# Operand pieces, background pieces, squares and first weights moved to other places in a two-layer trunk kernel

## The chip, the cores and the metric

The kernel runs on one core of a Trainium2 chip. The metric is the device time of one execution in microseconds (us). Engines go by the profile's names: PE is TensorE (PEld is its weight load), DVE is VectorE, ACT is ScalarE, POOL is GpSimd, SP is SyncE, which here issues the DMAs.

## The reference, cut to what matters

Two transformer-like layers over 1024 prompt tokens and 8 x 8 sample tokens, model width 1024, all in float32:

```
h = x
for layer in (0, 1):
    hn = rms_norm(h, norm_mix_g[layer])
    # layer 0: causal conv (width 31, LayerNorm, silu) | stick-breaking attention
    # layer 1: gated short conv                        | multi-scale causal pooling
    h = h + mixer(hn @ w_in) @ w_out
    g, u = split(rms_norm(h, norm_ffn_g[layer]) @ w_ffn_in[layer])      # 1024 -> 2 x 2816
    h = h + (silu(g) * u) @ w_ffn_out[layer]                            # 2816 -> 1024
y = rms_norm(h, norm_final_g)
```

The sample tokens have a cache of 1024 positions for the attention, gathered by a page table. Keys, values and the states of the convolutions and the pooling are outputs as well.

## The kernel before, in words

Activations lie transposed: channels on the partitions, tokens along the free axis. The 1088 tokens are two column groups, GA (0 to 511) and GB (512 to 1087, 576 columns). `hb` holds the residual stream in eight chunks of 128 channels.

**Matmuls.** Each float32 product is three products of split operands (high by high, high by low, low by high; `mm3`, L235). A *block* is one output chunk of 128 channels: eight input chunks of three products. PE does little else, and every block reads a 512 KB piece of weights that comes from memory just in time.

**Weights.** `w_load` (L166) has SP fetch a piece into `stage` (four buffers). `w_split` makes from it `hl` (three buffers): the high half by one ACT instruction (L184), the low half by two POOL subtractions (L186). In the FFN of group GB some pairs of channel pieces go by Strassen's scheme, seven products in place of eight; there DVE first forms sums of weights (L200 to L202), and ACT and POOL split those (L196, L197). `w_next` takes a piece and calls both for later ones.

**Order.** Nothing is scheduled by a tool; each engine runs its instructions in the order in which the code issues them. So that PE never waits, smaller work is put between its matmuls by hand. After each input chunk of a block a *slot* is called, and a slot takes the next piece of some other work:

- In layer 0, while GA goes through output projection (`run_out`) and FFN (`run_ffn`), slots take *background* pieces (`bg` from the list `flow`): the attention of GB (scores `z` L991, transposes `m` L1020, weighted sums `o` L1030 on PE; `q`, `be`, `kt` on DVE, L1005 to L1010 and L968; exponentials and copies on ACT), then the attention of the sample tokens and the convolution of GB. `drain` finishes what is left after GA's FFN.
- In layer 0, while GB goes through its FFN, slots take 21 *jobs* (`p0` to `p4` for four chunks, and a last cut), which form the sums and differences of GB's activations for the Strassen blocks: DVE lines L1466 to L1500, with a split of each by ACT and POOL (L1471). Once they are done, slots take pieces of the next layer's input (`ahead`) or GA's squares (`slot_d`). Those slots lie inside a block (`block(..., slot=slot)`, three a block), after a block (`slot()` in `one`), and between the blocks of the FFN's second matrix (`out_block`, 1.6 us each, which add to `hb` by DVE, L297).
- In layer 1, while GA goes through the FFN, every third slot takes a step of `forms_b`, which normalizes GB for its own FFN.

**The end of an output projection.** `run_out` does two chunks in a `pair` first, then four blocks, then chunks 6 and 7 in a `pair`. In this last pair each step also scales one finished chunk of `hb` for the FFN (`prep`: ACT L381, DVE L384 into `x`). `fin(n)` adds chunk n to `hb` (DVE L297) and its square to `ss` (`add_squares`: ACT L251, POOL L252). `norm_a` and `norm_b` make the root mean square's reciprocal from `ss`; the FFN's results are scaled by it afterwards (`rr`, DVE L293).

**A plain FFN block** ends in `acc` (PSUM, three buffers in GB's FFN). DVE scales it into `tmp` (L293), ACT applies silu, POOL or DVE multiplies, and ACT and DVE split the result into `hid` (L241).

**The start.** SP loads four pieces of x into `xt`; PE transposes them into `m` (L699), DVE copies them to `hb` (L705), ACT casts them (L381). The first weight is cast by ACT (L184) behind the first of these.

Of the kernel before, what the change touches and what calls it, by code (L numbers as in the profile page):

```python
# [57 lines left out]
def trunk_kernel(ctx, tc, x_prompt, x_sample, cache_k, cache_v, state_conformer, state_shortconv, state_pool,  # L58
# [261 lines left out]

    def pair(g, accs, x, ks, hooks, slot=None, skew=0, early=None):
        st = ((accs(), w_next()), (accs(), w_next(1)))
        for i in range(KC + skew):
            for (a, h), j in zip(st, (i, i - skew)):
                if 0 <= j < KC:
                    k = ks[j]
                    mm3(g, a, h[:, 0, k], h[:, 1, k], x[k], j == 0, j == KC - 1)
            if early and i == KC - 1:  # L330
                early(st[0][0])
            if i < skew:
                continue
            for f in hooks.get(k, []):
                f()
            if slot and j < KC - 1:
                slot()
        return st[0][0], st[1][0]

# [52 lines left out]
    def run_out(g, accs, x, gcol, ks=K0, slot=lambda: None, then=None):  # L392
        then = then or (g, x)

        def fin(n, a):
            added(g, hb[:, n, g.cs], a)
            add_squares(g, hb[:, n, g.cs], n == 0)

        a0, a1 = pair(g, accs, x, ks, {ks[0]: [flush]}, slot)
        w_split(wj[0] + 3)  # L400
        fin(0, a0)
        fin(1, a1)
        for n in range(2, 6):
            slot()
            h = w_next()
            a = accs()
            block(g, a, h, x, ks, slot=slot)
            w_split(wj[0] + 3)
            fin(n, a)
        slot()  # L410
        a0, a1 = pair(g, accs, x, K0, {k: [lambda k=k: prep(*then, k, pc(gcol + k)), lambda: low(0)]
                                       for k in range(6)}, slot, skew=2, early=lambda a: fin(6, a))
        w_split(wj[0] + 3)
        for n, a in ((6, a0), (7, a1)):
            if n == 7:
                fin(n, a)
            prep(*then, n, pc(gcol + n))
            low(1)
        low()
# [38 lines left out]


    def run_ffn(g, accs, ps, hidp, x, last, sig=False, slot=lambda: None, forms=None, plain=NF,  # L460
                free=lambda: None, hw=None, both=True):
        G = NF // 2
        n = g.n
        hid = {}
# [43 lines left out]
        def one(f, which):  # L508
            h = w_next()
            a = accs()  # L510
            block(g, a, h, x, K0[4:] + K0[:4] if done else K0, slot=slot)
            flush()
            ev_g(a) if which == 0 else ev_u(f, a)
            slot()
# [146 lines left out]
    def load_x(hf, t):  # L661
# [4 lines left out]
        else:  # L666
            sp.dma_start(xt[hf, t][:64], x_sample.rearrange("b q c -> (b q) c")[:, c])

    for hf in range(2):
        for t in range(4):  # L670
            load_x(hf, t)
        w_load(2 + hf)
# [752 lines left out]
    def slot_d():  # L1425
        turn[0] += 1
        if sq and turn[0] % 4 == 0:
            n = sq.pop(0)
            add_squares(GA, hb[:, n, GA.cs], n == 0)
# [21 lines left out]


    def make_forms(g, fp, gcol):
        def wide():
            assert "a" not in sums
            return fp.tile([128, 1024], F, name="sum1024")

        w2 = g.n // 2
        n1, n2 = slice(g.c0, g.c0 + w2), slice(g.c0 + w2, g.c1)
        l, r = slice(0, w2), slice(w2, g.n)  # L1460
        xs = [fp.tile([128, 3 * w2], F, name=f"xs{k}") for k in range(4)]
        tt = [[fp.tile([128, 2, g.n], FR, name=f"tt{k}_{i}") for i in range(2)] for k in range(4)]
        jobs = []

        def normed(out, c, cs):
            dve.scalar_tensor_tensor(out, hb[:, c, cs], pc(gcol + c), rr[:, cs], op0=OP.mult, op1=OP.mult)  # L1466

        def cut(k, i, x):
            o = tt[k][i]
            act.activation(o[:, 0], x[:, :g.n], AF.Copy)  # L1470
            pool.tensor_tensor(o[:, 1], x[:, :g.n], f32(o[:, 0]), op=OP.subtract)  # L1471

        box = {}

        def job(k):
            b21, b22, b11 = xs[k][:, l], xs[k][:, r], xs[k][:, g.n:]

            def p0():
                if k:
                    cut(k - 1, 1, box["u"])  # L1480
                normed(xs[k][:, 0:g.n], k + 4, g.cs)

            def p1():
                normed(b11, k, n1)

            def p2():
                t = box["t"] = tmp()
                normed(t[:, r], k, n2)
                dve.tensor_tensor(t[:, l], t[:, r], b11, op=OP.subtract)

            def p3():
                t, u = box["t"], wide()
                box["u"] = u
                dve.tensor_tensor(u[:, l], b22, t[:, r], op=OP.subtract)
                dve.tensor_tensor(t[:, r], b22, t[:, l], op=OP.subtract)

            def p4():
                t, u = box["t"], box["u"]
                cut(k, 0, t)
                dve.tensor_tensor(u[:, r], b21, t[:, r], op=OP.subtract)  # L1500
            return [p0, p1, p2, p3, p4]

        for k in range(4):
            jobs += job(k)
        jobs.append(lambda: cut(3, 1, box["u"]))

        def switch():
            while jobs:
                jobs.pop(0)()
            for k in range(4):  # L1510
                split(x1[4 + k][:, :, l], xs[k][:, g.n:])
            for k in range(4):
                split(x1[k][:, :, :g.n], xs[k][:, 0:g.n])

        forms = {"b21": lambda k: x1[k][:, :, l], "b22": lambda k: x1[k][:, :, r], "b11": lambda k: x1[4 + k][:, :, l],
                 "switch": switch}
        for i, (a, b) in enumerate((("t1", "t2"), ("t3", "t4"))):
            forms[a] = lambda k, i=i: tt[k][i][:, :, l]
            forms[b] = lambda k, i=i: tt[k][i][:, :, r]
        return forms, jobs  # L1520

    with tc.tile_pool(name="hid0b", bufs=2) as hidp:
# [17 lines left out]
        def slot_f():  # L1540
            if ahead:
                return ahead.pop(0)()
            if not jobs or wj[0] < jstart:
                return slot_d()
            jobs.pop(0)()

        jstart = wj[0] + 3
        run_ffn(GB, accs, ms, hidp, x1, to_mixer, slot=slot_f, forms=forms, plain=PLAIN, free=early)

    acc_pool(GT, 2)  # L1550

# [147 lines left out]

    def out_fin(g, n, a):  # L1700
        added(g, hb[:, n, g.cs], a)
        add_squares(g, hb[:, n, g.cs], n == 0)

    def normed(out, c, cs, view=lambda ap: ap):
        dve.scalar_tensor_tensor(out, view(hb[:, c, cs]), pc(FFNG + 8 + c), view(rr[:, cs]), op0=OP.mult, op1=OP.mult)
# [83 lines left out]


    def forms_b():
        dg = norm_a(GB, ms, D, xs[3])
        yield 1
        yield 1
        norm_b(GB, ms, dg)
        yield 1
        for k in range(4):
            normed(xs[k][:, 0:GB.n], k + 4, GB.cs)
            yield 1
            normed(xs[k][:, GB.n:], k, GB.cs)  # L1800
            yield 1
# [232 lines left out]
```

## Time and profile before

| | |
|---|---|
| time, median of three runs | 2506.31 us (2504.49 to 2506.65) |
| the profiled execution's own time | 2507.39 us |
| its span, first to last instruction | 2505.6 us |
| PE busy | 2420.9 us of the span |
| DVE, POOL, ACT busy | 1653.7, 1625.1, 1106.5 us |
| mean granted TensorE clock | 0.994 |

Times in the profile's rows are microseconds from the start of the span. In a row of the timeline come start, duration, engine, line, operation, output and inputs with their shapes, the count, and in brackets the idle time of the engine just before, with what ended it. In a row of windows come the window, its length, the busy time and count of PE, PEld, DVE, ACT and POOL, the granted clock, the share of the DMA engines and GB/s. The output projection of GA in layer 0 lies at about 330 to 430 us, the plain blocks of GB's FFN in layer 0 from about 1020, the output projection of GB in layer 1 ends at about 1728.

### The profile page before, as it was taken

The page shows a single profiled execution, that of the slowest core. Times are in us where ns is not written, and L with a number is a line of the kernel's source. Part 1 is how long each engine was busy: PE and PEld are TensorE (multiplying, and loading weights), DVE is VectorE, ACT ScalarE, POOL GpSimd, SP SyncE. Part 2 cuts the span into 40 slices and gives each one's busy share as a digit, 9 for nine tenths or more (in the row PEclk, how much of TensorE's full clock was granted, in tenths as well). Part 3 has the DMA queues.
Part 4 walks back from the last instruction along what each step waited for, and adds up shares of the span by engine and source line. Part 5 has one row for each costly group of instructions (what it writes and reads, how often), then busy time and mean ns, then how long its engine had stood idle before and what let it go on. Part 6 is the DMA issues. An engine that isn't in the chain of part 4 may idle for free.

```text
span 2505.6 us, 41453 instructions
## 1 busy us (share of the span) xinstructions
PE 2420.9 (97%) x15877; PEld 2190.0 (87%) x15877; DVE 1653.7 (66%) x2288; ACT 1106.5 (44%) x1877; POOL 1625.1 (65%) x1264
## 2 busy tenths in 40 slices
PE   8999999999999999999999999998999999999998
PEld 6788877788777679999999999888888888999998
DVE  3696878977777553766566534458777668666655
ACT  5536876754444343343333422234333444443333
POOL 6764334655654576787787523267888886887775
PEclk9999999999999999999999999999999999999999
DMA  7332231234565534223232311242233323233322
GB/s 226 117 108 73 77 111 48 72 103 144 175 180 172 160 93 148 71 74 98 89 100 86 111 49 43 71 139 68 85 101 102 98 90 92 85 98 114 93 85 81
DMA packets 355485, 258.31 MB, mean 103 GB/s; under 512 B 22913, under 2 KB 303617, under 8 KB 355272
## 3 DMA queue, kind: packets, MB, share of 16 engines
q1 hardware_dynamic: 355256, 255.66, 34.5%
q8 instruction: 126, 2.06, 0.3%
q14 instruction: 71, 0.58, 0.1%
q10 hardware_dynamic: 32, 0.01, 0.0%
HBM read 237.41 MB, written 18.69 MB: 102 GB/s over the span
## 4 chain that ended last, share of the span: by engine, by line
PE 73%; DVE 16%; POOL 4%; issue 3%; ACT 3%; DMA 1%; SPq 0%; DVEq 0%; ACTq 0%; POOLq 0%
PE acc L235 44%; PE acc L525 20%; DVE sum L200 1%; POOL hl L197 1%; DVE hb L297 1%; DVE q L1008 1%; POOL hl L186 1%; PE o L1030 1%; DVE hid L241 1%; PE m L1020 1%; PE m L1132 1%; PE z L991 1%; DVE sum L201 1%; PE z L1155 1%; DVE cacc L831 1%
## 5 line engine op out<-in xcount | busy, mean ns | idle before, releaser
L186 POOL TENSOR_TENSOR hl<-stage,hl 128x512 fp32r<-128x512 f32 x464 | 637.8, 1399 | 389.3 <-ACT hl L184 280.9
L235 PE MATMUL acc<-x,hl 128*128 128x512 f32 (+1 forms) x3648 | 773.5, 350 | 11.2 <-DVE tmp L293 3.0
L235 PEld LDWEIGHTS acc<-x,hl 128*128 128x128 f32 x3648 | 587.9, 190 | 75.1 <-issue 5.8
L235 PE MATMUL acc<-hid,hl 128*128 128x288 f32 (+1 forms) x3096 | 548.2, 333 | 10.8 <-DVE tmp L293 4.6
L235 PEld LDWEIGHTS acc<-hid,hl 128*128 128x128 f32 x3096 | 471.0, 189 | 62.9 <-DVE hb L297 7.2
L297 DVE TENSOR_TENSOR hb<-acc,hb 128x512 f32<-128x512 f32 (+1 forms) x360 | 256.3, 718 | 173.1 <-PE acc L235 171.7
L525 PE MATMUL acc<-x,hl 128*128 128x288 f32 (+1 forms) x2676 | 361.9, 290 | 3.0 <-POOL hl L197 2.4
L525 PEld LDWEIGHTS acc<-x,hl 128*128 128x128 f32 x2676 | 348.6, 188 | 5.3 <-POOL hl L197 3.3
L197 POOL TENSOR_TENSOR hl<-sum,hl 128x512 fp32r<-128x512 f32 x180 | 237.7, 1349 | 169.3 <-ACT hl L196 169.3
L184 ACT ACTIVATE hl<-stage 128x1024 fp32r<-128x1024 f32 x232 | 243.8, 1054 | 228.6 <-PE acc L235 145.8
L529 DVE TENSOR_TENSOR tmp<-acc,tmp 128x288 f32<-128x288 f32 (+1 forms) x420 | 173.6, 441 | 230.6 <-ACT tmp L541 136.2
L197 POOL TENSOR_TENSOR hl<-stage,hl 128x512 fp32r<-128x512 f32 x180 | 268.4, 1513 | 14.4 <-ACT hl L196 14.4
L525 PE MATMUL acc<-b,hl 128*128 128x256 f32 (+1 forms) x1548 | 215.7, 290 | 14.1 <-DVE tmp L529 11.2
L525 PEld LDWEIGHTS acc<-b,hl 128*128 128x128 f32 x1548 | 201.3, 188 | 19.8 <-ACT hl L196 12.6
L235 PE MATMUL acc<-x1t,hl 128*128 128x288 f32 x1152 | 216.3, 296 | 1.5 <-POOL hl L186 1.5
L235 PEld LDWEIGHTS acc<-x1t,hl 128*128 128x128 f32 x1152 | 195.9, 188 | 19.5 <-POOL hl L186 1.8
L196 ACT ACTIVATE hl<-sum 128x512 fp32r<-128x512 f32 x180 | 103.0, 623 | 238.1 <-DVE sum L202 217.6
L293 DVE TENSOR_TENSOR tmp<-acc,rr 128x512 f32<-128x512 f32 (+1 forms) x108 | 75.2, 710 | 136.3 <-PE acc L235 122.4
L196 ACT ACTIVATE hl<-stage 128x512 fp32r<-128x512 f32 x180 | 105.5, 618 | 69.4 <-PE acc L235 59.3
L504 POOL TENSOR_TENSOR tmp<-tmp 128x576 f32<-128x576 f32 (+1 forms) x85 | 126.2, 1485 | 9.2 <-ACT tmp L481 8.2
L252 POOL TENSOR_TENSOR ss<-ss,tmp 128x512 f32<-128x512 f32 (+1 forms) x69 | 108.1, 1566 | 25.5 <-ACT tmp L251 15.2
L235 PE MATMUL acc<-x1a,hl 128*128 128x512 f32 x480 | 121.7, 407 | 2.5 <-POOL hl L186 1.3
(298 smaller groups left out, 3166.5 us busy)
## 6 DMA issues: line engine op xcount, KB each, us to landing
stage<-in_w_ffn_in_dram SPq DMA_DIRECT2D x176, 512.0 KB
stage<-in_w_ffn_out_dram SPq DMA_DIRECT2D x88, 512.0 KB
stage<-in_w_in_even_dram SPq DMA_DIRECT2D x40, 512.0 KB
kst<-in_cache_k_dram SPq DMA_DIRECT2D x64, 256.0 KB
vst<-in_cache_v_dram SPq DMA_DIRECT2D x56, 256.0 KB
stage<-in_w_out_even_dram SPq DMA_DIRECT2D x16, 512.0 KB
stage<-in_w_in_odd_dram SPq DMA_DIRECT2D x16, 512.0 KB
stage<-in_w_out_odd_dram SPq DMA_DIRECT2D x16, 512.0 KB
```

What stands on the lines that cost most here:

```text
L184: act.activation(hl[:, 0], st, AF.Copy)
L186: pool.tensor_tensor(hl[:, 1, c], st[:, c], f32(hl[:, 0, c]), op=OP.subtract)
L196: act.activation(hl[:, 0, c], x, AF.Copy)
L197: pool.tensor_tensor(hl[:, 1, c], x, f32(hl[:, 0, c]), op=OP.subtract)
L200: todo = [lambda: dve.tensor_tensor(sb, su[:, lo], su[:, hi], op=OP.add), lambda: dve.tensor_tensor(sa[:, hi], sg[:, lo], su[:, lo], op=OP ...
L235: pe.matmul(acc[:, b, :c1 - c0], w, xs[:, xi, c0 - o:c1 - o], start=first and s == 0, stop=last and s == 2)
L252: pool.tensor_tensor(ss[:, g.cs], ss[:, g.cs], t[:, :g.n], op=OP.add)
L293: dve.tensor_tensor(d, a, r, op=OP.mult)
L297: dve.tensor_tensor(d, a, d, op=OP.add)
L504: (dve if both and f == NF - 1 else pool).tensor_tensor(t[:, :n], t[:, :n], u[:, :n], op=OP.mult)
L525: pe.matmul(acc[:, :w2], h[:, wi, i, k], xk[:, xi], start=k == 0 and s == 0, stop=k == 3 and s == 2)
L529: dve.tensor_tensor(out, acc[:, :w2], x, op=OP.add)
```

## The change

Five edits:

1. The first weight piece is loaded ahead of x: SP now issues one `stage` load, four of `xt`, a `stage`, four of `xt`, a `stage`, where four of `xt` came first and then two `stage` loads. The orders of ACT, DVE, POOL and PE at the start stay.
2. In the last pair of `run_out`, background pieces are taken in the first four steps and no longer in the last three (`quiet=3`). The three pieces come that much later, and all background behind them shifts by three slots.
3. In the same pair `sixth` issues the weight split of the piece after next ahead of `fin(6)`.
4. In the FFN of GB in layer 0 the jobs are taken only inside plain blocks (`inner=slot_j`); slots after a block or in the FFN's second matrix take other work. The jobs' scratch tile (`wide`) is now a part of `ss`.
5. In layer 1 the squares of GB's chunks 4 to 7 are left out of the output projection; `forms_b` does them, one in every third slot, from its second step on. `norm_a` and everything else in `forms_b` comes fifteen slots later.

```diff
-    def pair(g, accs, x, ks, hooks, slot=None, skew=0, early=None):
+    def pair(g, accs, x, ks, hooks, slot=None, skew=0, early=None, quiet=0):
...
-            if slot and j < KC - 1:
+            if slot and j < KC - 1 - quiet:
                 slot()
@@ run_out
+        def sixth(a):
+            w_split(wj[0] + 2)
+            fin(6, a)
...
         a0, a1 = pair(g, accs, x, K0, {k: [lambda k=k: prep(*then, k, pc(gcol + k)), lambda: low(0)]
-                                       for k in range(6)}, slot, skew=2, early=lambda a: fin(6, a))
+                                       for k in range(6)}, slot, skew=2, early=sixth, quiet=3)
@@ run_ffn, in one()
-            block(g, a, h, x, K0[4:] + K0[:4] if done else K0, slot=slot)
+            block(g, a, h, x, K0[4:] + K0[:4] if done else K0, slot=inner or slot)
@@ the start
+    w_load(1)
     for hf in range(2):
         for t in range(4):
             load_x(hf, t)
@@ make_forms
-        def wide():
-            assert "a" not in sums
-            return fp.tile([128, 1024], F, name="sum1024")
+        wide = ss[:, g.cs]
@@ FFN of GB, layer 0
         def slot_f():
             if ahead:
                 return ahead.pop(0)()
-            if not jobs or wj[0] < jstart:
-                return slot_d()
-            jobs.pop(0)()
+            slot_d()
+
+        def slot_j():
+            if jobs and wj[0] >= jstart:
+                jobs.pop(0)()
+            else:
+                slot_f()
@@ out_fin, layer 1
         added(g, hb[:, n, g.cs], a)
-        add_squares(g, hb[:, n, g.cs], n == 0)
+        if g is GA or n < 4:
+            add_squares(g, hb[:, n, g.cs], n == 0)
@@ forms_b
+        yield 1
+        for n in range(4, KC):
+            add_squares(GB, hb[:, n, GB.cs], False)
+            yield 1
         dg = norm_a(GB, ms, D, xs[3])
```

ACT at the end of GA's output projection in layer 0, before: `L996`, `L965`, `L966` and `L1021` are background, `L381` scales a chunk, `L251` squares one, and `L184` casts a weight.

```order
L996 ACTIVATE q_4165<-z_4160,bh 128x1024
L996 ACTIVATE be<-z_4160,bh 128x1024
L965 ACTIVATE kt<-kall 64x1024
L966 ACTIVATE qa<-hb 64x512
L251 ACTIVATE tmp<-hb 128x512
L381 ACTIVATE x_5_76<-hb,par 128x512
L1021 ACTIVATE wt_4190<-m 128x512
L1021 ACTIVATE wt_4190<-m 128x128
L996 ACTIVATE q_4205<-z_4200,bh 128x896
L996 ACTIVATE be<-z_4200,bh 128x896
L184 ACTIVATE hl<-stage 128x1024 x2
```

The same place after the change:

```order
L381 ACTIVATE x_4_75<-hb,par 128x512
L184 ACTIVATE hl<-stage 128x1024
L251 ACTIVATE tmp<-hb 128x512
L381 ACTIVATE x_5_76<-hb,par 128x512
L184 ACTIVATE hl<-stage 128x1024
L381 ACTIVATE x_6_77<-hb,par 128x512
L251 ACTIVATE tmp<-hb 128x512
L381 ACTIVATE x_7_78<-hb,par 128x512
```

The background's rows are gone from between the last scalings, and one weight cast stands ahead of the square and scaling of the sixth chunk.

DVE in the FFN of GB in layer 0, before: `L293` evacuates a plain block, `L1466` to `L1500` are jobs, `L241` splits a hidden piece, `L297` evacuates the eight parts of the second matrix.

```order
L1466 SCALAR_TENSOR_TENSOR xs_10840<-hb,par,rr 128x576
L1466 SCALAR_TENSOR_TENSOR xs_10840<-hb,par,rr 128x288
L1466 SCALAR_TENSOR_TENSOR tmp<-hb,par,rr 128x288
L1489 TENSOR_TENSOR tmp<-tmp,xs_10840 128x288
L1494 TENSOR_TENSOR sum_11307<-xs_10840,tmp 128x288
L1495 TENSOR_TENSOR tmp<-xs_10840,tmp 128x288
L293 TENSOR_TENSOR tmp<-acc,rr 128x576
L1500 TENSOR_TENSOR sum_11307<-xs_10840,tmp 128x288
L241 TENSOR_TENSOR hid<-tmp,hid 128x576
L293 TENSOR_TENSOR tmp<-acc,rr 128x576
L297 TENSOR_TENSOR hb<-acc,hb 128x576 x8
```

After the change (job lines are now L1468 to L1501):

```order
L1468 SCALAR_TENSOR_TENSOR xs_10840<-hb,par,rr 128x576
L1468 SCALAR_TENSOR_TENSOR xs_10840<-hb,par,rr 128x288
L1468 SCALAR_TENSOR_TENSOR tmp<-hb,par,rr 128x288
L1491 TENSOR_TENSOR tmp<-tmp,xs_10840 128x288
L241 TENSOR_TENSOR hid<-tmp,hid 128x576
L293 TENSOR_TENSOR tmp<-acc,rr 128x576
L297 TENSOR_TENSOR hb<-acc,hb 128x576 x8
L200 TENSOR_TENSOR sum_11514<-stage 128x512
L201 TENSOR_TENSOR sum_11513<-stage 128x512
L202 TENSOR_TENSOR sum_11513<-sum_11514,stage 128x512
L1495 TENSOR_TENSOR ss<-xs_10840,tmp 128x288
L1496 TENSOR_TENSOR tmp<-xs_10840,tmp 128x288
```

The last three jobs of the fourth chunk now come behind the eight parts of the second matrix, and four job rows stand between two evacuations where six stood.

POOL at the end of GB's output projection in layer 1, before: `L252` adds a square to `ss`, `L186` and `L197` make the low halves of weights.

```order
L252 TENSOR_TENSOR ss<-ss,tmp 128x576
L186 TENSOR_TENSOR hl<-stage,hl 128x512 x2
L252 TENSOR_TENSOR ss<-ss,tmp 128x576
L197 TENSOR_TENSOR hl<-sum_17599,hl 128x512 x2
L252 TENSOR_TENSOR ss<-ss,tmp 128x576
L197 TENSOR_TENSOR hl<-sum_17600,hl 128x512
L197 TENSOR_TENSOR hl<-stage,hl 128x512
L252 TENSOR_TENSOR ss<-ss,tmp 128x576
L197 TENSOR_TENSOR hl<-stage,hl 128x512 x2
L252 TENSOR_TENSOR ss<-ss,tmp 128x576
L197 TENSOR_TENSOR hl<-sum_c,hl 128x512
```

After, further on in the FFN of GA (L508 there is a product of hidden values):

```order
L252 TENSOR_TENSOR ss<-ss,tmp 128x576
L197 TENSOR_TENSOR hl<-stage,hl 128x512 x2
L508 TENSOR_TENSOR tmp<-tmp 128x512
L197 TENSOR_TENSOR hl<-sum_c,hl 128x512
L186 TENSOR_TENSOR hl<-stage,hl 128x512 x4
L252 TENSOR_TENSOR ss<-ss,tmp 128x576
L508 TENSOR_TENSOR tmp<-tmp 128x512
L197 TENSOR_TENSOR hl<-sum_18249,hl 128x512 x2
L252 TENSOR_TENSOR ss<-ss,tmp 128x576
L197 TENSOR_TENSOR hl<-sum_18250,hl 128x512
L197 TENSOR_TENSOR hl<-stage,hl 128x512
L252 TENSOR_TENSOR ss<-ss,tmp 128x576
```

The four squares that stood between the last weights of the projection now stand between weights of the FFN.

More of the change, by code (lines that the diff above doesn't have):

```diff
@@ L460, in run_ffn @@
     def run_ffn(g, accs, ps, hidp, x, last, sig=False, slot=lambda: None, forms=None, plain=NF,
-                free=lambda: None, hw=None, both=True):
+                free=lambda: None, hw=None, both=True, inner=None):
         G = NF // 2
@@ L1479, in p0 @@
                 if k:
-                    cut(k - 1, 1, box["u"])
+                    cut(k - 1, 1, wide)
                 normed(xs[k][:, 0:g.n], k + 4, g.cs)
@@ L1491, in p3 @@
             def p3():
-                t, u = box["t"], wide()
-                box["u"] = u
+                t, u = box["t"], wide
                 dve.tensor_tensor(u[:, l], b22, t[:, r], op=OP.subtract)
@@ L1497, in p4 @@
             def p4():
-                t, u = box["t"], box["u"]
+                t, u = box["t"], wide
                 cut(k, 0, t)
@@ L1504, in make_forms @@
             jobs += job(k)
-        jobs.append(lambda: cut(3, 1, box["u"]))
+        jobs.append(lambda: cut(3, 1, wide))
         def switch():
@@ L1542, in slot_f @@
                 return ahead.pop(0)()
-            if not jobs or wj[0] < jstart:
-                return slot_d()
-            jobs.pop(0)()
+            slot_d()
[4 more added lines that the diff above has]
+                slot_f()
         jstart = wj[0] + 3
-        run_ffn(GB, accs, ms, hidp, x1, to_mixer, slot=slot_f, forms=forms, plain=PLAIN, free=early)
+        run_ffn(GB, accs, ms, hidp, x1, to_mixer, slot=slot_f, forms=forms, plain=PLAIN, free=early,
+                inner=slot_j)
     acc_pool(GT, 2)
```

## The prediction

> **What bounds the kernel now.** I read the busy shares and the chain of waits first, then the idle gaps of PE along the timeline, and at each gap the rows of the engine that ended it.
>
> ```profile
> PE 2420.9 (97%) x15877; PEld 2190.0 (87%) x15877; DVE 1653.7 (66%) x2288; ACT 1106.5 (44%) x1877; POOL 1625.1 (65%) x1264
> PE 73%; DVE 16%; POOL 4%; issue 3%; ACT 3%; DMA 1%; SPq 0%; DVEq 0%; ACTq 0%; POOLq 0%
> ```
>
> PE is busy for 2420.9 of 2505.6 us, so all its gaps together are 85 us, and the edits touch no matmul. What they can win is gaps, and time in which the clock is granted at half. The sum is made against the profiled execution (2507.39 us), which is 1.08 us above the median; I subtract it from the median, 2506.31. What a measurement can tell from no change is about 0.2%, 5.0 us.
>
> **Edit 1, first weight ahead of x.**
>
> ```profile
> 0.75 1.83 SPq L665 DMA_DIRECT2D xt<-in_x_prompt_dram  x4
> 2.62 1.07 SPq L166 DMA_DIRECT2D stage<-in_w_in_even_dram  x2
> 7.72 2.38 PE L699 MATMUL m<-ident,xt 128*128 128x128 f32 x9 [0.43 <-DMA xt<-in_x_prompt_dram]
> 8.23 0.69 DVE L705 COPY hb<-m 128x512 f32<-128x512 f32 x1 [4.02 <-PE m L699]
> 8.96 0.72 ACT L381 ACTIVATE x1a<-hb,par 128x512 fp32r<-128x512 f32 x1 [6.71 <-DVE hb L705]
> 10.10 1.04 ACT L184 ACTIVATE hl<-stage 128x1024 fp32r<-128x1024 f32 x1
> 11.23 5.42 POOL L186 TENSOR_TENSOR hl<-stage,hl 128x512 fp32r<-128x512 f32 x4 [8.91 <-ACT hl L184]
> 2.00:8.00 6.00, 1.89 (x6) 1.00 (x7) 0.17 (x1) 0.23 (x2) 0.32 (x1) 1.00 0.90 265
> ```
>
> The chain is x by DMA, transposes at 7.72, DVE, ACT, then the weight cast at 10.10, which shows no wait: the weight is there, it stands behind x on ACT. ACT's order does not change, so an earlier weight helps nobody, while x comes behind 512 KB more. From 2 to 8 us memory delivers 265 GB/s at 0.90 of the DMA engines, so 524288 bytes take 1.98 us. If the transfers share the engines in order, x, the cast and the first matmuls all come that much later. Ends: 0 (the two overlap so well that x's last piece ends as before, since 0.10 of the engines are free) and +3.5 (1.98, and a weight POOL gets later still, 1.5 for a slower start of the clock, an estimate from the half-clock price below). I take **+1.8**, close to the row's 1.98. The other loads at the start move by one place, behind them.
>
> **Edits 2 and 3, the end of GA's output projection.**
>
> ```profile
> 415.37 2.08 DVE L1008 TENSOR_TENSOR_SCAN q<-q,ones 128x896 f32<-128x896 f32 x1
> 417.11 0.73 PE L235 MATMUL acc<-x,hl 128*128 128x512 f32 x2 [1.25 <-ACT hl L184]
> 417.55 2.05 DVE L1010 TENSOR_TENSOR be<-be,q 128x1023 f32<-128x1023 f32 x1
> 418.58 3.55 PE L235 MATMUL acc<-x,hl 128*128 128x512 f32 x14 [0.73 <-POOL hl L186]
> 419.62 3.37 DVE L968 TENSOR_TENSOR kt<-kall,kt 64x512 fp32r<-64x512 f32 x2
> 423.63 1.03 DVE L384 SCALAR_TENSOR_TENSOR x<-hb,par,x 128x512 fp32r<-128x512 f32 x1
> 424.72 4.31 PE L235 MATMUL acc<-x,hl 128*128 128x512 f32 x11 [2.60 <-DVE x L384]
> 424.60:427.90 3.30, 3.18 (x8) 2.50 (x9) 1.39 (x2) 1.67 (x2) 1.20 (x1) 0.50 0.54 159
> ```
>
> DVE does three pieces of background (2.08 + 2.05 + 3.37 = 7.50 us) back to back from 415.37 to 423.0, and the low half of the scaled chunk (L384, 423.63), for which PE waits 2.60, comes behind them. The casts for which PE waits 1.25 and, through POOL, 0.73 stand on ACT behind the background's exponentials. Behind the 2.60 the clock is at 0.50 for 3.4 us, which costs half of it, 1.7. With the three pieces gone from here and the cast put ahead, all of that can go: 1.25 + 0.73 + 2.60 + 1.7 = 6.28.
>
> The pieces are not gone but later. PE's part of them is as long there. Their DVE part, 7.50, enters a stretch where each piece takes the place of its successor, and at the end of the background three slots, empty before, are filled.
>
> ```profile
> 440.00:460.00 20.00, 19.31 (x136) 15.80 (x135) 19.49 (x13) 17.29 (x28) 19.49 (x15) 1.00 0.35 97
> 877.00:897.00 20.00, 20.00 (x86) 15.80 (x85) 9.18 (x12) 8.68 (x13) 16.78 (x12) 1.00 0.27 79
> 465.02 1.25 PE L1020 MATMUL m<-ident,be 128*128 128x128 f32 x7 [2.76 <-DVE be L1010]
> ```
>
> Where the attention runs, DVE is busy for 19.49 of 20 us and PE still for 19.31; where the background ends, DVE has 20 - 9.18 = 10.82 free and PE has no gap. So the cover of the 7.50 is that end; without it the cost is up to 7.50. I take the 0.69 that PE loses in 20 us of dense background, since three slots more of it are less than that long. Net **-5.6** (ends: -6.3, and +1.2 with all 7.50 paid). That all later pieces meet other matmuls I put at 0, with the stall at 465.02 (2.76) as the kind of thing that may go or come.
>
> [...]
>
> The same `sixth` in GB's output projection, where no background runs: 0.
>
> **Edit 4, jobs inside plain blocks.**
>
> ```profile
> 1034.23 1.52 DVE L1494 TENSOR_TENSOR sum<-xs,tmp 128x288 f32<-128x288 f32 x1 [1.32 <-POOL tt L1471]
> 1056.28 0.75 DVE L293 TENSOR_TENSOR tmp<-acc,rr 128x576 f32<-128x576 f32 x1
> 1057.09 1.86 PE L235 MATMUL acc<-hid,hl 128*128 128x288 f32 x12 [1.03 <-DVE tmp L293]
> 1061.71 0.75 DVE L293 TENSOR_TENSOR tmp<-acc,rr 128x576 f32<-128x576 f32 x1
> 1062.51 11.37 PE L235 MATMUL acc<-hid,hl 128*128 128x288 f32 x72 [3.57 <-DVE tmp L293]
> 1062.90:1066.20 3.30, 3.30 (x16) 3.30 (x15) 1.56 (x3) 0.00 (x0) 3.30 (x4) 0.50 0.56 164
> ```
>
> A plain block leaves its accumulator to DVE (L293), three accumulators go round, and DVE comes late because job pieces queue ahead of L293. When the second matrix begins, whose blocks are short, PE has run out of accumulators twice: 1.03 and 3.57, and behind the second gap the clock is at 0.50 for 3.4 us, again 1.7. Together 6.3. After the change no job follows a block or sits between out parts, six job rows between two evacuations become four, and the last three jobs go behind the second matrix's first eight parts. I take the second gap and its half clock as gone (3.57 + 1.7 = 5.3) and leave the 1.03, since four job rows still stand ahead of L241 and the last L293 there: **-5.3**. Ends: 0 (DVE is as late as before) and -6.3. The job total is the same 21, and the 1.32 that DVE waits for POOL (the scratch tile) may go with `wide`; I count neither. `ss` in place of an own tile adds a wait only if GB's square sum is still read, which the norm ahead of the FFN is done with: 0. Squares of GA and `ahead` that now take the freed slots are as many as before: 0.
>
> **Edit 5, squares of layer 1.**
>
> ```profile
> 1717.67 1.44 PE L525 MATMUL acc<-x,hl 128*128 128x256 f32 x10 [0.27 <-POOL hl L197]
> 1718.81 1.89 POOL L252 TENSOR_TENSOR ss<-ss,tmp 128x576 f32<-128x576 f32 x1
> 1722.42 1.44 PE L525 MATMUL acc<-x,hl 128*128 128x256 f32 x10 [1.66 <-POOL hl L197]
> 1724.04 1.42 POOL L252 TENSOR_TENSOR ss<-ss,tmp 128x576 f32<-128x576 f32 x1
> 1726.75 1.46 PE L525 MATMUL acc<-b,hl 128*128 128x256 f32 x10 [0.92 <-POOL hl L197]
> L252 POOL TENSOR_TENSOR ss<-ss,tmp x4: 1422/1660/1885, 1708.1 to 1724.0; 128x576 f32<-128x576 f32 x4
> 1740.55 1.66 PE L525 MATMUL acc<-b,hl 128*128 128x256 f32 x12 [2.73 <-DVE tmp L529]
> 1750.00:1800.00 50.00, 46.68 (x328) 42.58 (x327) 35.61 (x52) 21.55 (x37) 44.89 (x33) 1.00 0.34 101
> ```
>
> Four squares of 1.66 us, 6.64 in all, stand on POOL ahead of weight halves for which PE then waits 0.27 + 1.66 + 0.92 = 2.85: gone. They are repaid in the FFN, where POOL has 50 - 44.89 = 5.11 us free in 50; 6.64 - 5.11 = 1.53 does not fit if they fall into such a stretch. I take +1.5 (ends 0, when a buffer of slack hides them, and +6.64). The wait of 2.73 at 1740.55, behind `norm_a`'s DVE work, moves with `norm_a`: 0, within 2.73 either way. Its reader comes late enough: `forms_b` now ends some 48 slots into an FFN of over 110. Net **-1.35**.
>
> **Sum.** +1.8 - 5.6 - 5.3 - 1.35 = -10.45: 2506.31 - 10.45 = **2495.9 us**. In the profiled execution that would be 2496.9.
>
> **The rivals.**
>
> *The pieces are paid back in full.* For it: DVE at 97% in the attention, where nothing more fits, and the stall at 465.02. Against: 10.82 us free where the background ends. Then edits 2 and 3 give +1.2 in place of -5.6: 2502.7, within the bound. Chance 0.15.
>
> *The jobs still hold DVE.* For it: the same 21 jobs, the same three accumulators, fewer slots for them, so that they come denser. Against: they leave the last evacuations. Edit 4 gives 0: 2501.2, at the edge of the bound. Chance 0.10.
>
> *The moved squares are exposed.* POOL is at 44.89 of 50 us and PE waits for it.
>
> ```profile
> 1708.63 1.92 DVE L201 TENSOR_TENSOR sum<-stage 128x512 f32<-128x512 f32 x1
> 1738.33 0.68 DVE L201 TENSOR_TENSOR sum<-stage 128x512 f32<-128x512 f32 x1
> ```
>
> The same DVE sum takes 1.92 beside POOL's square and 0.68 without, so a moved square can hold up DVE's weight sums as well, which stand ahead of POOL's cuts. All 6.64 paid in place of 1.5: 2501.0. Against: three buffers of split weights lie between POOL and PE, and PE idles 3.32 of these 50 us already. Chance 0.12. [...]
>
> *Slower: the background's new phase makes new stalls.* Each like 465.02: 2.76 of gap and, if the half clock follows, 1.7, so 4.46. The background is some 450 us long with every piece against other matmuls. Three new ones give 2495.9 + 13.4 = 2509.3; it decides from the fourth, 2495.9 + 17.8 = 2513.7. Against: the pieces stand in the same order and PE lost 0.69 in 20 us where DVE was densest. Chance 0.07.
>
> *More than forecast.* The stall at 465.02 and the 1.03 go too, and x is not delayed: 2495.9 - 4.5 - 1.0 - 1.8 = 2488.6. Chance 0.08.
>
> **How the numbers follow.** The forecast has 0.48. Faster than 2501.3: 0.48 + 0.08 + half of the two rivals at the edge, (0.10 + 0.12) / 2 = 0.11, together 0.67. Within: 0.15 + 0.11 = 0.26. Slower: 0.07. The range, 2487 to 2504.5, takes in the better case and the first three rivals, and leaves out the slower one and what lies past the ends. The forecast's own range, from the ends of its terms that are likeliest, is 2492 to 2500.
>
> **What would show it.** Edit 1: the transposes start near 9.7 in place of 7.72, the cast stays without a wait. Edits 2 and 3: between 415 and 430 no gap of PE over 0.5 and a granted clock of 1.00; DVE's L384 right behind L297. Edit 4: the wait for L293 ahead of the second matrix is about 1, with no half clock. Edit 5: no wait for L197 in the projection's last 12 us; POOL busier between 1740 and 1790, PE's busy share there no less than 46.68 of 50. The prediction is wrong if the wait for DVE moves along with the pieces (new gaps of over 2 us between 430 and 880), or if the gap ahead of the second matrix only shifts.

## The result, and the profile after

The changed kernel takes 2524.57 us (median of six runs, 2521.91 to 2526.51) beside 2506.48 for the kernel before; the ratio is 1.0068, 95% interval 1.0059 to 1.0078. Forecast was 2495.9. The profiled execution took 2524.89 us, its span is 2523.1.

To see where the 18 us lie I use *marks*: the n-th matmul of the foreground (one that writes `acc`) is the same work in both kernels, so the difference of its start in two traces is what has been lost up to there. Between marks 1600 and 3200 background stands in between, so only the two ends are compared.

| mark | start before | after, later by | what lies ahead of it |
|---|---|---|---|
| 0 | 11.19 | 0.99 | start |
| 1600 | 399.06 | 2.76 | first layer up to GA's output projection |
| 3200 | 944.86 | 20.90 | its end, GA's FFN with all background |
| 4800 | 1171.58 | 17.09 | the jobs in GB's FFN |
| 8000 | 1672.61 | 17.13 | rest of layer 0, mixer of layer 1 |
| 8400 | 1731.90 | 12.12 | the squares' old place |
| 13400 | 2463.36 | 17.52 | the squares' new place, rest |

So in this pair of traces the start costs 1 to 3, the jobs win 3.8, the squares win 5.0 and give 5.4 back (1.0 of each is the ten matmuls of `norm_a`, which lie ahead of mark 8400 before and behind it after), and edits 2 and 3, which were to win 5.6, lose 18.1. There the tail itself did what was forecast, nearly: one gap of 1.81 is left, and the clock stays whole. The timeline of PE and the window, kernel after:

```profile
415.46 7.40 PE L235 MATMUL acc<-x,hl 128*128 128x512 f32 x27 [1.81 <-DVE hb L297]
415.00:430.00 15.00, 14.48 (x86) 10.65 (x87) 7.56 (x13) 7.95 (x11) 6.18 (x4) 1.00 0.23 66
```

The loss is in the attention that follows. First the window from 430 to 580 and the transposes' group in it (busy, mean ns, idle ahead and who ended it), before:

```profile
430.00:580.00 150.00, 145.57 (x912) 119.61 (x911) 121.49 (x125) 96.03 (x160) 84.77 (x73) 0.99 0.32 94
L1020 PE MATMUL m<-ident,be 128*128 128x128 f32 x130 | 18.6, 281 | 4.2 <-DVE be L1010 3.7 <-POOL be L998 0.4
L991 PE MATMUL z<-kt,qa 128*128 128x384 f32 (+3 forms) x36 | 14.4, 402 | 0.3 <-ACT be L996 0.3
```

The same after (L1020 is now L1025, L991 is L996):

```profile
430.00:580.00 150.00, 134.65 (x827) 109.54 (x826) 108.38 (x99) 91.79 (x154) 73.97 (x69) 0.94 0.24 68
L1025 PE MATMUL m<-ident,be 128*128 128x128 f32 x135 | 20.5, 294 | 12.6 <-ACT wt L1026 11.6 <-DVE be L1015 1.0
L996 PE MATMUL z<-kt,qa 128*128 128x448 f32 (+3 forms) x39 | 16.5, 425 | 2.8 <-ACT be L1001 2.8
```

PE waits 12.6 + 2.8 = 15.4 us where it waited 4.2 + 0.3, and nearly all of it for ACT's copy of the transposes (`wt`), which ended no wait here before. The granted clock is 0.94 in place of 0.99: stretches at half clock (0.50) fill 17.1 of the 150 us in place of 3.4. I count them as costing half their length, 6.8 more. That is an estimate from the clock, and an upper one: 128x512 matmuls, one right behind the other, start every 427 ns in such stretches of both traces and every 234 ns at full clock (medians), which makes it 0.45 of the length. Over the whole of marks 1600 to 3200, with the tail's gain in it, PE idles 28.2 us in place of 16.9 and half clock costs 10.2 in place of 3.4: 11.3 + 6.8 = 18.1, by this estimate the whole loss. The first such wait, in the timelines of DVE, ACT and PE after:

```profile
441.50 2.67 DVE L1013 TENSOR_TENSOR_SCAN q<-q,ones 128x768 f32<-128x768 f32 x1
444.30 1.87 DVE L1015 TENSOR_TENSOR be<-be,q 128x895 f32<-128x895 f32 x1
446.10 0.68 DVE L293 TENSOR_TENSOR tmp<-acc,rr 128x512 f32<-128x512 f32 x1
446.87 0.63 ACT L482 ACTIVATE tmp<-tmp 128x512 f32<-128x512 f32 x1 [7.08 <-DVE tmp L293]
447.40 0.54 ACT L1038 ACTIVATE hb<-o 64x128 f32<-64x128 f32 x2
447.97 1.08 ACT L1026 ACTIVATE wt<-m 128x512 f32<-128x512 f32 x2
448.62 1.75 PE L1025 MATMUL m<-ident,be 128*128 128x128 f32 x7 [5.17 <-ACT wt L1026]
473.58 0.63 ACT L482 ACTIVATE tmp<-tmp 128x512 f32<-128x512 f32 x1 [6.32 <-DVE tmp L293]
475.46 1.66 PE L1025 MATMUL m<-ident,be 128*128 128x128 f32 x7 [2.52 <-ACT wt L1026]
```

Read upwards: the transposes wait for a buffer that ACT's copy frees; the copy stands on ACT behind the sigmoid of a gate block (L482); the sigmoid waits 7.08 for the gate's evacuation (L293); and that stands on DVE behind the background's scan and product. ACT idles all this time with the copy next but one in its queue. 26.8 us later the same happens again, at 500.89 a third time (2.45) and at 548.09 a last time (1.47); at 525.67, between them, PE waits 0.95 for DVE.

Why it recurs is seen in the code. GB's attention yields twice for each of a head's four units, so a head takes 8 slots. GA's FFN has 4 slots for each of the four blocks of two hidden chunks and 8 between the parts of the second matrix: 24, three heads. A head therefore meets the same places of the FFN again and again, and a shift by three slots is kept for the whole attention.

### The profile page after: what moved, and what is told of

It reads as the page before. It is cut to its first block, busy times and chain, and to the rows that moved or that the text cites. A ratio compares the mean times of both kernels' runs of the same rounds, so it can differ in the third digit from the quotient of the medians.

```text
span 2523.1 us, 41423 instructions
## 1 busy us (share of the span) xinstructions
PE 2428.5 (96%) x15877; PEld 2195.9 (87%) x15877; DVE 1664.7 (66%) x2288; ACT 1102.0 (44%) x1877; POOL 1623.1 (64%) x1264
## 4 chain that ended last, share of the span: by engine, by line
PE 70%; DVE 16%; ACT 3%; POOL 3%; issue 2%; DMA 0%; SPq 0%; DVEq 0%; ACTq 0%; POOLq 0%
PE acc L235 43%; PE acc L529 20%; POOL hl L197 2%; DVE q L1013 2%; DVE hb L297 1%; DVE sum L200 1%; DVE be L1015 1%; PE m L1137 1%; PE z L1160 1%; PE o L1035 1%; DVE sum L201 1%; DVE hid L241 1%; PE z L996 1%; PE m L1025 1%; DVE q L1010 1%
## 5 line engine op out<-in xcount | busy, mean ns | idle before, releaser
L186 POOL TENSOR_TENSOR hl<-stage,hl 128x512 fp32r<-128x512 f32 x464 | 634.9, 1392 | 431.8 <-ACT hl L184 319.6
L297 DVE TENSOR_TENSOR hb<-acc,hb 128x512 f32<-128x512 f32 (+1 forms) x360 | 256.4, 718 | 172.1 <-PE acc L235 170.6
L529 PE MATMUL acc<-x,hl 128*128 128x288 f32 (+1 forms) x2676 | 361.7, 290 | 4.4 <-DVE tmp L533 2.2
L529 PEld LDWEIGHTS acc<-x,hl 128*128 128x128 f32 x2676 | 349.0, 188 | 6.3 <-POOL hl L197 2.2
L197 POOL TENSOR_TENSOR hl<-sum,hl 128x512 fp32r<-128x512 f32 x180 | 236.8, 1343 | 160.9 <-ACT hl L196 160.9
L184 ACT ACTIVATE hl<-stage 128x1024 fp32r<-128x1024 f32 x232 | 243.6, 1054 | 212.0 <-PE acc L235 136.7
L197 POOL TENSOR_TENSOR hl<-stage,hl 128x512 fp32r<-128x512 f32 x180 | 269.3, 1517 | 12.6 <-ACT hl L196 12.6
L529 PE MATMUL acc<-b,hl 128*128 128x256 f32 (+1 forms) x1548 | 216.3, 291 | 11.2 <-DVE tmp L533 8.6
L529 PEld LDWEIGHTS acc<-b,hl 128*128 128x128 f32 x1548 | 202.2, 189 | 16.7 <-ACT hl L196 9.8
L293 DVE TENSOR_TENSOR tmp<-acc,rr 128x512 f32<-128x512 f32 (+1 forms) x108 | 75.1, 709 | 132.1 <-PE acc L235 110.7
L508 POOL TENSOR_TENSOR tmp<-tmp 128x576 f32<-128x576 f32 (+1 forms) x85 | 127.8, 1504 | 9.4 <-ACT tmp L485 9.3
L252 POOL TENSOR_TENSOR ss<-ss,tmp 128x512 f32<-128x512 f32 (+1 forms) x69 | 108.7, 1575 | 19.8 <-ACT tmp L251 17.0
```

Of the source, the lines that this page charges most:

```text
L184: act.activation(hl[:, 0], st, AF.Copy)
L186: pool.tensor_tensor(hl[:, 1, c], st[:, c], f32(hl[:, 0, c]), op=OP.subtract)
L197: pool.tensor_tensor(hl[:, 1, c], x, f32(hl[:, 0, c]), op=OP.subtract)
L252: pool.tensor_tensor(ss[:, g.cs], ss[:, g.cs], t[:, :g.n], op=OP.add)
L293: dve.tensor_tensor(d, a, r, op=OP.mult)
L297: dve.tensor_tensor(d, a, d, op=OP.add)
```

## The experiments

All ratios are against the kernel before, timed on the same chip, where it took 2507.3 to 2507.6 us. Where an expectation speaks of marks, it means those above.

**e1, the changed kernel with the pieces back in the tail.** Its edit:

```diff
-  slot, skew=2, early=sixth, quiet=3)
+  slot, skew=2, early=sixth, quiet=0)
```

> The changed kernel with the background taken to the end of the last pair again (quiet=0); its other edits stay. Phase theory: in GB's attention a head takes 8 slots, and the FFN of GA has 24 slots for every two chunks, so a shift of three slots is kept for the whole attention and puts each head's longest DVE work ahead of the same evacuation every time. Taking the shift back gives back what foreground matmul 1600 to 3200 lost (2.8 behind at 399 us, 20.9 behind at 945 us): 18 less, 2506.5 us. Rival, the weight split put ahead of fin(6) or the later start is the cause: it stays above 2520.

Measured: 2506.01 us, ratio 0.9996 (0.9987 to 1.0005). The 18 us are gone; from mark 1600 to 3200 it loses 1.9. So `quiet=3` is what cost them, and neither the order of the weight split nor the later start.

**e2, the shift alone.** The tail keeps its pieces; three slots of the FFN stay empty:

```diff
+    skip = [3]
+    def bg_ffn():
+        if skip[0]:
+            skip[0] -= 1
+            return
+        bg()
-    run_ffn(GA, accs, ms, hidp, x1, last_a, sig=True, slot=bg, both=False)
+    run_ffn(GA, accs, ms, hidp, x1, last_a, sig=True, slot=bg_ffn, both=False)
```

> The kernel before with one thing added: the first three slots of GA's FFN are left empty, so the background is three slots late and the end of the output projection keeps all its pieces. Phase theory: the stalls of the changed kernel come here without any other edit, and the tail's waits stay too: before plus 16 to 24, 2522 to 2530 us. Rival, the 7.5 us of DVE work that the tail no longer does are what is paid: here the tail does them, so before plus 0 to 3, 2506 to 2509 us.

Measured: 2521.34 us, ratio 1.0058 (1.0044 to 1.0072), a little under what the phase theory named and far from its rival. Group of the transposes and window, 430 to 580:

```profile
L1020 PE MATMUL m<-ident,be 128*128 128x128 f32 x130 | 19.0, 286 | 8.7 <-ACT wt L1021 7.7 <-DVE be L1010 1.0
430.00:580.00 150.00, 138.88 (x855) 112.60 (x854) 110.62 (x107) 89.21 (x150) 77.26 (x68) 0.95 0.28 80
```

The same wait for ACT's copy, and the same low clock, with no piece moved out of the tail.

**e3, e8, e11: shifts of eight, four and six.** The kernel before with `quiet=3` and five, one or three empty slots behind it:

```diff
-  slot, skew=2, early=lambda a: fin(6, a))
+  slot, skew=2, early=lambda a: fin(6, a), quiet=3)
...
+    skip = [5]        # e8: [1], e11: [3]; bg_ffn as in e2
```

> The kernel before with quiet=3 and the next five slots of the FFN empty: a shift of eight slots, one whole head. Phase theory: each head meets the same foreground as before, so the tail's gain is kept (4.6 of gaps and perhaps 1.7 of half clock): 2500 to 2503 us. Rival, what counts is how much background is pushed back: eight slots cost more than three, above 2524 us.

> The kernel before with quiet=3 and one empty slot in the FFN: a shift of four slots, half a head, so that gate and up blocks change places against the heads. Phase theory: another phase has another price, and nothing says that it lies near that of three; if the price comes from the gate's evacuation behind the head's longest DVE rows, it is far from three's: 2500 to 2512 us. Rival, any shift that puts pieces out of the tail costs what the changed kernel costs: 2520 or more.

> The kernel before with quiet=3 and three empty slots: a shift of six. Phase theory: a price of its own, the same at each head, which three, four and eight slots (about 16, 3 and 1 us over before by the marks at 945 us) do not give; gaps should recur at one place of a head, every 26 us or so. If price grew with the number of pieces pushed back, it would lie between those of four and eight: 2508 to 2510.

Measured: eight 2508.19 (1.0001; 0.9992 to 1.0010), four 2510.70 (1.0015; 1.0005 to 1.0024), six 2516.39 (1.0030; 1.0018 to 1.0042). From mark 1600 to 3200 they lose 1.1, 2.6 and 10.2 us; three slots cost 18.1 (after) and 14.8 (e2). The price does not grow with the number of pieces pushed back: eight cost least, four much less than three. A whole head brings the old phase back, but the tail's gain does not show in e3; its expectation missed by 5 to 8 us. These three kernels have no `sixth`, and in their tails the wait of 2.60 for DVE's L384 is gone, but one of 1.97 for the cast of a weight is there, with a stretch of half clock behind it (the granted clock is 0.94 from 400 to 430; e3, PE):

```profile
414.24 0.73 PE L235 MATMUL acc<-x,hl 128*128 128x512 f32 x2 [1.97 <-ACT hl L184]
```

In the phase of six another wait recurs, every 25 us (451.74, 477.81, 502.91): the transposes wait for DVE itself.

```profile
L1020 PE MATMUL m<-ident,be 128*128 128x128 f32 x141 | 21.2, 292 | 10.7 <-DVE be L1010 10.7
```

**e7, the chain cut at ACT.** The changed kernel, its phase untouched; only the sigmoid of a gate is issued one block later, with the other postponed work:

```diff
-                s = tmp()
-                act.activation(s[:, :n], t[:, :n], AF.Sigmoid)
-                pool.tensor_tensor(t[:, :n], t[:, :n], s[:, :n], op=OP.mult)
+                def silu():
+                    s = tmp()
+                    act.activation(s[:, :n], t[:, :n], AF.Sigmoid)
+                    pool.tensor_tensor(t[:, :n], t[:, :n], s[:, :n], op=OP.mult)
+                post.append(silu)
```

> The changed kernel, but the sigmoid of a gate block (ACT L482) and its product on POOL are issued one block later, with the other postponed work; phase and edits stay. Theory of the queue: the transposes wait for the copies L1026 because these stand on ACT behind the sigmoid, which waits for DVE's late evacuation L293. Then the waits for L1026 and L1001 go (5.17 + 2.52 + 0.40 + 2.45 + 1.03 + 1.47 + 1.03 = 14.1): 2510 to 2514 us. Rival, DVE itself is late and the transposes wait for its be (L1015) instead: 2520 or more.

Measured: 2505.95 us, ratio 0.9994 (0.9984 to 1.0003), 18.6 below the changed kernel and better than either theory named, since the half clocks go with the waits (0.99 in place of the changed kernel's 0.94 in the window). Group and window, 430 to 580 (L1027 is the transposes):

```profile
L1027 PE MATMUL m<-ident,be 128*128 128x128 f32 x135 | 18.8, 277 | 8.4 <-DVE be L1017 8.4
430.00:580.00 150.00, 141.46 (x894) 116.11 (x893) 124.63 (x116) 97.67 (x162) 83.48 (x74) 0.99 0.31 88
```

No wait for ACT is left, and the clock is back at 0.99. DVE still holds PE for 8.4 us in this phase, over twice what it did in the old one. From mark 1600 to 3200 it loses 4.9 in place of 18.1.

**e6, the pieces caught up.** The changed kernel, with two pieces in each of the FFN's first three slots; behind them all is in the old phase:

```diff
+    twice = [3]
+    def bg_ffn():
+        bg()
+        if twice[0]:
+            twice[0] -= 1
+            bg()
```

> The changed kernel, but each of the first three slots of GA's FFN takes two pieces, so that from there on every piece stands where it stood before. Phase theory: the stalls between 430 and 880 go, 16 to 20 us less: 2504 to 2508 us, with the tail still free of its wait. Rival, the 7.5 us of DVE work moved out of the tail is what has to be paid: it now falls even denser, so no better than 2515.

Measured: 2503.56 us, ratio 0.9983 (0.9974 to 0.9992), 21 below the changed kernel. But from mark 1600 to 3200 it gains only 0.2. Timeline of PE:

```profile
430.94 0.47 PE L996 MATMUL z<-kt,qa 128*128 128x448 f32 x1 [1.27 <-ACT be L1001]
434.76 1.31 PE L1035 MATMUL o<-wt,vrow 128*64 128x128 f32 x20 [0.97 <-ACT wt L1026]
442.86 1.41 PE L1025 MATMUL m<-ident,be 128*128 128x128 f32 x7 [3.66 <-DVE be L1015]
```

Here PE idles 1.27 + 0.97 + 3.66 = 5.9 us within some 15 us of the tail's end, while the 2.76 at 465.02 does not come again. Over marks 1600 to 3200 PE idles 18.2 us in place of 16.9, and half clock costs 1.7 in place of 3.4. This reads as if the waits in the tail were the price of doing these pieces near that time, and not of doing them in that place; no run tests it further.

**e12, the weight split ahead, alone.** The kernel before with `sixth` and nothing else:

```diff
+        def sixth(a):
+            w_split(wj[0] + 2)
+            fin(6, a)
-  slot, skew=2, early=lambda a: fin(6, a))
+  slot, skew=2, early=sixth)
```

> The kernel before with edit 3 alone (the weight split ahead of fin(6)). In e1, which has it, the tail shows one gap of 6.07 behind DVE's L384 in place of 1.25 + 0.73 + 2.60 = 4.58, and the marks lose 1.7 there: the waits for the weight go and DVE's wait takes them over and more: before plus 0 to 2, 2507 to 2509 us. Rival, the forecast's reading that the cast's waits of 1.98 just go: 2505.

Measured: 2508.28 us, ratio 1.0005 (0.9995 to 1.0014): no change that can be told. Its tail, DVE and PE:

```profile
421.97 2.25 DVE L972 TENSOR_TENSOR kt<-kall,kt 64x512 fp32r<-64x512 f32 x2
424.26 0.69 DVE L297 TENSOR_TENSOR hb<-acc,hb 128x512 f32<-128x512 f32 x1
424.87 0.74 DVE L384 SCALAR_TENSOR_TENSOR x<-hb,par,x 128x512 fp32r<-128x512 f32 x1
425.66 2.93 PE L235 MATMUL acc<-x,hl 128*128 128x512 f32 x6 [6.08 <-DVE x L384]
```

The weight's waits (1.25 and 0.73) are gone, and one wait of 6.08 for DVE is in their place, where 2.60 stood. DVE ends its pieces when it did.

**e4, the jobs alone.** Edit 4 on the kernel before, all its lines as in the change's diff, of which the one that decides is

```diff
-            block(g, a, h, x, K0[4:] + K0[:4] if done else K0, slot=slot)
+            block(g, a, h, x, K0[4:] + K0[:4] if done else K0, slot=inner or slot)
```

> The kernel before with edit 4 alone (jobs inside plain blocks, scratch in ss). The marks of the two traces say that this stretch gained 3.8 us (20.9 behind at 1029.8, 17.1 at 1145): 2502.5 us. Rival, that gain belongs to the other state in which the changed kernel came there: 2506 us.

Measured: 2501.26 us, ratio 0.9982 (0.9973 to 0.9991): faster. Over this stretch (marks 3200 to 4800) the seven profiled kernels with the edit gain 2.3 to 4.0 against before, and the six others lie between 0.2 gained and 1.4 lost. The seven fall into two groups: 2.3 to 2.5 where a stretch of half clock falls into these marks (e1, e4, e6), 3.8 to 4.0 where none does (after, e7, e9, e10). What is left is best seen in the kernel after:

```profile
1080.39 2.80 PE L235 MATMUL acc<-hid,hl 128*128 128x288 f32 x19 [1.83 <-DVE tmp L293]
1110.40 1.91 DVE L214 TENSOR_TENSOR sum_c<-stage,sum 128x512 f32<-128x512 f32 x1
1114.56 1.84 PE L529 MATMUL acc<-x,hl 128*128 128x288 f32 x12 [1.97 <-DVE tmp L533]
1058.00:1090.00 32.00, 30.17 (x227) 29.93 (x226) 25.28 (x26) 11.91 (x16) 27.80 (x20) 1.00 0.27 83
```

The gap of 3.57 is gone, and in this kernel its half clock too; in e1 and e4 half clock comes right behind the same gap of 1.83 and 1.82 (where these gaps lie, the last section says). The first gap grew from 1.03 to 1.83, and ahead of the first Strassen evacuations, where 0.42 was lost, 1.97 is.

**e5, the squares alone.** Edit 5 on the kernel before:

```diff
-        add_squares(g, hb[:, n, g.cs], n == 0)
+        if g is GA or n < 4:
+            add_squares(g, hb[:, n, g.cs], n == 0)
...
+        yield 1
+        for n in range(4, KC):
+            add_squares(GB, hb[:, n, GB.cs], False)
+            yield 1
```

> The kernel before with edit 5 alone (four squares of layer 1 moved into the FFN). By the marks of the matmuls in the profiles so far, the squares win 5.0 where they leave (17.1 to 12.1 behind around 1720 us) and lose up to 5.4 in the FFN in the changed kernel, 3.2 in the kernel with quiet=0: before minus 0 to 2, 2505 to 2507 us. Rival, paid back in full or more: above 2508.

Measured: 2506.51 us, ratio 0.9992 (0.9983 to 1.0001): a gain of 1 to 2, not told from none. From mark 8000 to 8400 it wins 5.0, from there to 13400 it loses 3.4. Of the 5.0, 1.0 only moves: `norm_a`'s ten matmuls, which stood here before, now come behind mark 8400:

```profile
1730.86 1.17 PE L259 MATMUL m<-ones,ss 128*128 128x1 f32 x10
```

In the kernel after, the new place reads so (windows and POOL, PE):

```profile
1750.00:1800.00 50.00, 44.53 (x301) 40.63 (x301) 36.05 (x45) 21.22 (x37) 47.42 (x34) 0.97 0.27 81
1793.21 1.88 POOL L252 TENSOR_TENSOR ss<-ss,tmp 128x576 f32<-128x576 f32 x1
1796.80 1.45 PE L529 MATMUL acc<-x,hl 128*128 128x256 f32 x10 [1.81 <-POOL hl L197]
```

The last square stands directly ahead of the weight halves for which PE then waits 1.81.

**e9 and e10, two versions from what was learnt.** e9 is the kernel before with edits 4 and 5 and the sigmoid of e7; e10 is e6 without edit 1 and with that sigmoid:

```diff
-    w_load(1)         # e10, against e6
...
+                post.append(silu)        # both, as in e7
```

> The kernel before with edits 4 and 5 and the sigmoid of e7, without edits 1 to 3. By the marks of the profiled runs the jobs give 2.4 and the squares 1.6, and the sigmoid nothing, since in the old phase the transposes wait for DVE's be (465.02, 2.76) and not for ACT's copies: before minus 4, 2503 us. Rival, the sigmoid on ACT costs or wins in every phase: 2 to 5 more either way.

> e6 (three pieces caught up in the FFN's first three slots) without edit 1 and with the sigmoid of e7. e6 was 2503.6; its start is 0.7 later than without edit 1 (mean of the marks of four and six profiles), and of its waits at 430 to 443 us 0.97 is for ACT's copy, which may go: 2501 to 2503 us. Rival, the three doubled slots hold DVE whatever ACT does: 2503 or more.

Measured: e9 2500.50, ratio 0.9975 (0.9964 to 0.9987); e10 2501.34, ratio 0.9977 (0.9968 to 0.9986). By their medians both beat the kernel before by 6 to 7 us and the changed one by 23 to 24, and they cannot be told from each other. In e9 marks 1600 to 3200 gain 3.0, but that is not shown to be the sigmoid: PE idles 17.0 us there, as before (16.9), and what is missing are the two stretches of half clock at 424.57 and 465.53 (3.4). By the ratios e4 and e5 alone give 0.9982 x 0.9992 = 0.9974, all that e9 has; so nothing that can be told is left for the later sigmoid in the old phase, as was expected.

## Why the prediction was wrong, point by point

**The step that failed** is in edits 2 and 3: "That all later pieces meet other matmuls I put at 0, with the stall at 465.02 (2.76) as the kind of thing that may go or come." It is the slower rival that came true: the shift costs 14.8 us by itself (e2). That rival was priced as separate accidents of 4.46 each, four of which would be needed. They are not separate. A head has 8 slots and the FFN's cycle 24, so one bad meeting comes again with the next heads (5.17, 2.52, 2.45 and 1.47 us of wait for ACT's copy), and the chance of several was the chance of one. The one stall that the profile showed, at 465.02, spoke of DVE; the chain through ACT's queue was not on the page, and could have been found only by asking what stands behind L482 once L293 comes late. e7 shows that chain: issuing the sigmoid and its product a block later, in the bad phase, returns 18.6 us, 13.3 of them in this stretch by the marks.

**The tail.** The waits went as forecast, except for 1.81 in place of 0. But the rival of a full payback came true as well: even in the old phase, in e6, PE idles 5.9 us right behind the tail, and the net is 0.2. "So the cover of the 7.50 is that end" named the wrong cover. The free DVE time at 877 us belongs to slots 450 us later, and the pieces that came late were wanted at 430.

**The weight split ahead** was not worked out by itself; alone it turned two waits into a longer one (e12), and without it, with the pieces gone, the wait for the cast stays (1.97 in e3).

**Edit 1.** Forecast +1.8. The first weight matmul starts 0.99 later, the last transposes at 8.71 in place of 7.72 (forecast near 9.7), and the cast shows no wait, as said:

```profile
8.71 2.37 PE L704 MATMUL m<-ident,xt 128*128 128x128 f32 x9 [0.26 <-DMA xt<-in_x_prompt_dram]
11.09 1.99 ACT L184 ACTIVATE hl<-stage 128x1024 fp32r<-128x1024 f32 x2
```

Mark 0 lies at +0.37 to +0.99 in the four profiles that have the edit, and from -0.95 to +0.96, mean -0.12, in the ten without it. The direction is likely right, the size 0.8 rather than 1.8, and the spread of the loads is as large. It was not timed alone, and e6 and e10, which differ by it and by the sigmoid, lie within each other's intervals, so this term stays open.

**Edit 4.** The mechanism was right. The size, -5.3, is too large by the marks (-2.3 to -4.0); the runs, -0.0018 x 2507 = -4.5 (2.3 to 6.8), do not exclude it. By the traces the term was mis-sized at "leave the 1.03", which became 1.83, by the new 1.97 that the sum put at 0, and by a half clock that was counted as gone for good and still comes in some traces.

**Edit 5.** The sum came out near: -1.35 forecast, -1.6 by the marks of e5, -2.0 by its runs, which do not exclude 0. The old place did as forecast: PE's idle time between marks 8000 and 8400 falls from 4.05 to 1.21, 2.84 for 2.85. The new place took more than the 1.5: between marks 8400 and 13400 PE's waits for weight halves (POOL L197) grow from 1.96 to 4.88 us in e5 and to 3.70 in the changed kernel. The largest of them there, 1.81, stands behind a square directly ahead of the weights, on a POOL that is busy for 47.42 of 50 us. That `norm_a` moves too was put at 0; its wait of 2.73 for DVE is gone from 1740.55, and waits for DVE's `tmp` (L529) fall from 11.19 to 8.49 in e5. In the changed kernel's trace the 5.0 is lost again whole, half clock included: three stretches of it lie behind mark 8400 where one did before.

## What to carry to other kernels

When background work is fed into slots of a foreground loop, compare the two periods before moving anything: where one divides the other, a shift is a choice of phase that is paid again and again, and its price is found by measuring several shifts, not by counting the work moved. An instruction that waits for another engine should not be issued, on one engine, ahead of one that frees a buffer for the busiest engine (ACT stood idle for 7.08 us here with that copy next but one); issuing it later won back 18.6 us in the one bad phase where it was tried, and nothing that can be told in the old one. And work taken out of a stretch that waits for an engine at its limit was no gain here, where that engine had room only long after the work was due.

## What the runs showed of the hardware

In these traces the granted clock did not go by the length of one gap. Before, a gap of 1.31 was followed by a granted clock that averages 0.66 over 5 us; after, 5.17 was followed by 0.50, while 1.81 (415.46) and 1.83 (1080.39) were followed by 1.00, in windows quoted above. Before and after:

```profile
331.67 0.49 PE L235 MATMUL acc<-x,hl 128*128 128x512 f32 x1 [1.31 <-ACT x L240]
331.00:336.00 5.00, 4.09 (x12) 3.15 (x13) 4.35 (x8) 5.00 (x10) 0.00 (x0) 0.66 0.49 138
```

```profile
449.00:452.50 3.50, 3.19 (x13) 2.69 (x12) 2.46 (x3) 3.45 (x6) 0.15 (x2) 0.50 0.00 0
```

The traces' records of the granted clock show more. In all fourteen traces a stretch of half clock lasts 3.41 us or twice that (but for the one at the end of the execution, 7.76 before and 8.37 after), and within a trace all of them begin whole steps of 3.413 us apart (before: 332.41, 356.31, 424.57, 465.53 and 1062.87 are 7, 20, 12 and 175 steps apart). Cut into these steps, the records of these traces go with how long PE idles in one step, all gaps together. Before and after, from 35 us on, 1430 steps are at full clock: half clock followed all 12 with 1.90 us of idle or more, none of the 1397 with less than 1.30, and 8 of the 21 between. Over all fourteen traces (9996 steps) it followed all 52, none of 9801, and 37 of 143; what decides among those between is open. So in these traces a gap of one length was followed by half clock or not by where it lay. The 1.31 above shares its step with smaller gaps, 1.80 of idle together. The 2.60 behind which the prediction saw half clock lies mostly in one step before (PE busy 0.96 of 3.41), and is split over two in e9:

```profile
421.16:424.57 3.41, 0.96 (x5) 0.43 (x3) 3.38 (x4) 0.82 (x2) 3.01 (x3) 1.00 0.53 154
424.57:427.98 3.41, 3.26 (x8) 2.58 (x9) 1.42 (x2) 1.70 (x2) 1.23 (x1) 0.50 0.53 154
425.47 2.90 PE L235 MATMUL acc<-x,hl 128*128 128x512 f32 x10 [2.60 <-DVE x L384]
421.32:424.73 3.41, 1.55 (x7) 0.93 (x5) 3.38 (x4) 0.24 (x1) 3.41 (x3) 1.00 0.52 152
424.73:428.14 3.41, 2.64 (x10) 1.89 (x11) 2.02 (x2) 2.29 (x3) 1.43 (x2) 1.00 0.54 156
```

The 1.82 of e4 lies in one step and the 1.83 of the kernel after in two. Counted at half its length, one stretch of 3.41 is 1.7 us (an estimate, as above): a difference of that size between the marks of two single traces can be no more than this.
